# The affine part of the first layer norm computed on GpSimd beside the key scores and kept in DRAM

## The chip, the cores and the metric

The kernel runs on one core of a Trainium2 chip. A core has TensorE (PE in the profile, with its weight loads as PEld), VectorE (DVE), ScalarE (ACT), GpSimd (POOL) and SyncE (SP, which here only issues DMAs). Each engine works through its own queue in order and waits on semaphores. The metric is the device time of one execution in microseconds, lower is better; the median of the runs is what counts.

## What is computed

One layer of a diffusion backbone: differential attention over 512 latent and 256 context tokens, a layer norm, a PEER feed-forward with 16,384 experts, and a second layer norm. Cut to what matters here:

```python
h = layer_norm(DN_ALPHA * h + g1 * o, ln_g[i, 0], ln_b[i, 0])       # o: attention
f = peer_ffn(h * (1.0 + sc2) + sh2, peer_wq[i], peer_keys[i], peer_u[i], peer_v[i])
h = layer_norm(DN_ALPHA * h + g2 * f, ln_g[i, 1], ln_b[i, 1])

def layer_norm(x, g, b):
    mu, var = mean(x), mean((x - mu) ** 2)
    return (x - mu) * rsqrt(var + LN_EPS) * g + b
```

`peer_ffn` scores each token against two sets of 128 sub-keys per head (8 heads), takes the best 16 of each, then the best 16 sums, and mixes the chosen experts. The `h` that enters the second line's norm is the first norm's full output, with its scale `g` and shift `b`: the affine part that this case is about. It is needed only in the last line.

## The kernel before, in words

The 512 tokens are four tiles of 128 (t = 0 to 3), with the 1024 features along a row. Every f32 product is made of three matmuls on a high and a low part (`hi_lo`, lines 135 to 139: ACT writes the high part, DVE or GpSimd the low one; `mm3`, lines 141 to 150).

- `mix` (line 658) makes the first norm. `normed(t)` writes the normed rows without scale and shift to the DRAM tensor `nd[t]`, 512 KB each (line 711).
- `scores` (line 855) is a loop over 16 sets of keys (k). A step has 24 matmuls of 512 columns on weights `qhi`, `qlo`; from k = 4 on GpSimd makes `qlo` (line 882), from weights that SP loads into `qraw` (line 866, two buffers). DVE takes the best 16 of four tiles (`top16`: MAX8, FIND_INDEX8, MATCH_REPLACE8). After step 1 the pool `ag` is made, with five row buffers named `gr`, 512 KB each.
- Tiles 0 to 2 then go through all experts densely (`up`, `down`); tile 3 has its 128 chosen experts gathered one by one into the five `gr` buffers (`fetch` on GpSimd, `gather` on DVE, which adds into `facc`).
- `down` (line 1131) runs over j = 0 to 127, 128 experts each. `prepare(j)` makes the parts `vh`, `vl` (from `vr`) and `wh`, `wl` (from `w`): the high ones on ACT, the low ones on DVE. `accumulate(j)` is 18 matmuls into six PSUM banks. The last five j (TM = 5) are multiplied bank by bank, so that `finish` of a tile can begin while the next is still multiplied: 90 matmuls.
- When the last gather of tile 3 is out, near j = 117, `finish` for tile 3 is put into the queues: `last_rows` loads four rows of norm parameters (scale and shift of both norms, broadcast to 128 partitions) into `gr` buffers, `residual` loads `nd[3]` into the fifth and has GpSimd multiply by the first norm's scale and add its shift (lines 1221, 1222). Tiles 0 to 2 do the same in buffers `h`. `finish` then makes `y = ALPHA * y + gate * f` on DVE (lines 1232, 1233) and the second norm, half of whose affine part is again on GpSimd (lines 1239, 1240; not for tile 2).

A scheduler orders the instructions of each queue, with dependences and priorities of its own; some are pinned to the order in which they are written (`Pinned`, `pin`). A buffer is taken again when its last reader is done, so the load into a `gr` buffer waits for the `gather` that used it.

Of the kernel before, what the change touches and what calls it, by code (L numbers as in the profile page):

```python
# [9 lines left out]
F32 = mybir.dt.float32  # L10
# [10 lines left out]
D = 1024  # L21
# [81 lines left out]
class Net:  # L103
# [5 lines left out]
    def build(self):  # L109
        with ExitStack() as es:  # L110
            self.es = es
            tc = self.tc
            self.cp = es.enter_context(tc.tile_pool(name="cp", bufs=1))
            self.pinned = {}
            self.V = Pinned(self, self.nc.vector)
            self.A = Pinned(self, self.nc.scalar)
            self.T = Pinned(self, self.nc.tensor)
            self.consts()
            for phase in (self.attention, self.mix, self.peer):
                phase()  # L120
                if self.stop == phase.__name__ or self.stop == "route" and phase == self.peer:
                    break
            if self.stop == "attention":
                self.wh.release()
                self.wpool.release()
                self.onpool.release()
            if self.stop == "mix":
                self.u2p.release()
# [529 lines left out]
    def mix(self):  # L658
# [6 lines left out]
        ps = es.enter_context(tc.tile_pool(name="mps", bufs=1, space=PSUM, reuse_waits="tile"))  # L665
        self.dram = self.es.enter_context(tc.tile_pool(name="dram", bufs=1, space=bass.MemoryType.DRAM))
        self.nd = self.dram.tile([NT, 128, D], F32, name="nd")
        self.keys = self.u2p.tile([128, 2, 128], F32, name="keys")
        nc.sync.dma_start(self.keys, a["keysT"])

# [184 lines left out]
    def scores(self):  # L855
# [4 lines left out]
        with tc.tile_pool(name="qp", bufs=1, reuse_waits="tile") as qp:  # L860
# [17 lines left out]
            def split(k):  # L878
                if k < 2 * H:
                    S[k] = [qp.tile([128, KB, 128], FR, name=x, bufs=2) for x in ("qhi", "qlo")]  # L880
                    self.A.activation(S[k][0], RAW[k], AF.Copy)
                    (nc.vector if k < 4 else nc.gpsimd).tensor_tensor(S[k][1], RAW[k], S[k][0].bitcast(F32), op=OP.subtract)  # L882
                    load(k + 2 if k > 3 else 16)

            def product(k):
# [8 lines left out]
            for k in range(2 * H):  # L894
# [14 lines left out]
                if k == 1:  # L909
                    for kb in range(KB):  # L910
                        self.T.transpose(self.row2[:, kb * 128:(kb + 1) * 128], self.u3[:, kb], self.ident)
                    for n in range(2):
                        self.A.activation(self.u2t[:, 512 * n:512 * n + 512], self.row2[:, 512 * n:512 * n + 512], AF.Copy)
                    self.wh.release()
                    self.wpool.release()
                    self.onpool.release()
                    self.ag = self.pes.enter_context(tc.tile_pool(name="ag", bufs=1, side="right", reuse_waits="tile"))
                    self.ug = tc.alloc_tile_pool(name="ug", bufs=1, side="right", reuse_waits="tile")

    def choose(self, t, then=None):  # L920

# [209 lines left out]
    def down(self):  # L1131
# [47 lines left out]

        for j in range(128 - TM):  # L1180
            if at(j - 1) == 256 and not row:
                row += self.last_rows()
                skip[DT] = self.residual(self.ag.tile([128, D], F32, name="gr", bufs=5), DT, row)
                self.finish(self.ag, row, skip, DT, [self.facc[:, :512], self.facc[:, 512:]])
            prepare(j + 2)
            for t in range(DT):
                accumulate(j, t)
            if j + AHEAD in fresh:
                self.up(j + AHEAD)
            self.some(at(j + 1))  # L1190
# [5 lines left out]
        for j in range(130 - TM, 128):  # L1196
            prepare(j, fp if j > 130 - TM else None)
        for t in range(DT):
            skip[t] = self.residual(fp.tile([128, D], F32, name="h", bufs=3), t, row)
        for t in range(DT):  # L1200
            for n in range(2):
                for j in range(128 - TM, 128):
# [3 lines left out]
        vp.release()  # L1206
        ap.release()

    def last_rows(self):

        row = []
        for n in range(4):
            row.append(self.ag.tile([128, D], F32, name="gr", bufs=5))
            self.nc.sync.dma_start(row[n], self.a["ln"][n:n + 1].to_broadcast([128, D]))
        return row

    def residual(self, h, t, row):

        nc = self.nc
        nc.sync.dma_start(h, self.nd[t])  # L1220
        nc.gpsimd.tensor_tensor(h, h, row[0], op=OP.mult)
        nc.gpsimd.tensor_tensor(h, h, row[1], op=OP.add)
        return h

    def finish(self, fp, row, skip, t, f):
# [9 lines left out]
        for i in range(2):  # L1235
            ns = slice(512 * i, 512 * i + 512)
            if i == 1 and t != DT - 1:
                nc.scalar.activation(y[:, ns], y[:, ns], AF.Identity, bias=bias, scale=scale)
                nc.gpsimd.tensor_tensor(y[:, ns], y[:, ns], row[2][:, ns], op=OP.mult)
                nc.gpsimd.tensor_tensor(y[:, ns], y[:, ns], row[3][:, ns], op=OP.add)  # L1240
            else:
                nc.vector.scalar_tensor_tensor(y[:, ns], y[:, ns], mean, row[2][:, ns], op0=OP.subtract, op1=OP.mult)
                nc.vector.scalar_tensor_tensor(y[:, ns], y[:, ns], rstd, row[3][:, ns], op0=OP.mult, op1=OP.add)
            nc.sync.dma_start(self.out[0, t * 128:(t + 1) * 128, ns], y[:, ns])


# [70 lines left out]
```

## Time and profile before

| | |
|---|---|
| median of 3 runs | 1704.1 us (1698.33, 1704.1, 1705.66) |
| the profiled execution, its time | 1702.72 us |
| its span (first to last instruction) | 1700.9 us |
| mean granted TensorE clock | 0.98 of full speed |
| PE busy | 1608.8 us (95%) |
| DVE busy | 1462.5 us (86%) |
| ACT busy | 761.8 us (45%) |
| POOL busy | 646.2 us (38%) |

The rows of the trace are in microseconds from the start of the span. A row of the timeline has the start, the duration, the engine, the line, the operation, what it writes and reads, and in brackets how long the engine had been idle before and what ended that. A helper's instructions carry the helper's line (L97 for those that are pinned, L138 and L139 for `hi_lo`, L146, L148, L149 for the three matmuls of `mm3`). Matmuls are pipelined: the distance between two starts is what one costs, not its duration.

### The profile page before, as it was taken

What the parts mean: (1) busy time and instruction counts of PE and PEld (TensorE: products, weight loads), DVE (VectorE), ACT (ScalarE), POOL (GpSimd) and SP (SyncE); (2) the same over time, 40 slices, a digit from 0 to 9 for tenths busy, and PEclk for the clock granted to TensorE, in tenths of its full rate; (3) what the DMA queues carried; (4) which work ended last, traced back from release to release, by engine and by line L of the source; (5) the groups of instructions that cost most, each with busy time, mean ns of one, the idle gap of its engine ahead of it and who ended that gap; (6) DMA issues with size and microseconds to landing.
All of it is one profiled execution on the core that took longest, in us unless ns stands there. A gap on an engine that the chain in (4) does not pass through costs nothing.

```text
span 1700.9 us, 24498 instructions
## 1 busy us (share of the span) xinstructions
PE 1608.8 (95%) x9057; PEld 1430.2 (84%) x9057; DVE 1462.5 (86%) x2598; ACT 761.8 (45%) x1148; POOL 646.2 (38%) x368
## 2 busy tenths in 40 slices
PE   7899999997999999899999979999999999999977
PEld 3788897876888998899999968888888888888865
DVE  6688897887799999999999468989899789888978
ACT  5475656654333343564666533333333333333322
POOL 1000000000234676327333235655566556655552
PEclk9999999998999999899999989999999999999988
DMA  8765746403222566798999999989899889988952
GB/s 317 192 173 153 180 130 177 151 21 127 89 86 73 177 224 206 266 347 266 333 367 340 331 359 360 378 319 374 322 376 360 336 331 372 362 333 296 356 193 97
DMA packets 134920, 435.92 MB, mean 256 GB/s; under 512 B 13200, under 2 KB 38288, under 8 KB 123408
## 3 DMA queue, kind: packets, MB, share of 16 engines
q1 hardware_dynamic: 75328, 201.02, 34.7%
q0 software_dynamic: 36864, 134.23, 21.2%
q10 hardware_dynamic: 22608, 99.10, 16.6%
q8 instruction: 71, 1.16, 0.3%
q14 instruction: 49, 0.40, 0.1%
HBM read 372.57 MB, written 47.05 MB: 247 GB/s over the span
## 4 chain that ended last, share of the span: by engine, by line
PE 77%; DVE 9%; DMA 6%; issue 4%; ACT 2%; POOL 2%; SPq 0%; ACTq 0%; DVEq 0%; POOLq 0%
PE v L149 11%; PE v L146 10%; PE v L148 10%; PE a L149 10%; PE a L146 10%; PE a L148 9%; PE v L97 3%; PE qkv L146 2%; PE qkv L149 2%; PE qkv L148 2%; DMA adw<-in_ada_b_dram 2%; PE sc L409 2%; DMA qs<-kh 1%; PE mp L228 1%; POOL ulo L1019 1%
## 5 line engine op out<-in xcount | busy, mean ns | idle before, releaser
L146 PE MATMUL a<-u2h,uhi 128*128 128x384 f32 x1024 | 346.7, 339 | 4.5 <-ACT at L97 2.8
L149 PE MATMUL a<-u2h,ulo 128*128 128x384 f32 x1024 | 344.9, 337 | 6.2 <-POOL ulo L1019 4.5
L148 PE MATMUL a<-u2l,uhi 128*128 128x384 f32 x1024 | 343.9, 336 | 0.0
L146 PE MATMUL v<-vh,wh 128*128 128x512 f32 x768 | 300.9, 392 | 9.8 <-ACT wh L138 9.8
L148 PE MATMUL v<-vl,wh 128*128 128x512 f32 x768 | 301.7, 393 | 8.1 <-DVE vl L139 8.1
L149 PE MATMUL v<-vh,wl 128*128 128x512 f32 x768 | 301.7, 393 | 4.6 <-DVE wl L139 4.5
L1095 POOL DMA_INDIRECT gr<-in_peer_u_dram,eidx x128 | 184.3, 1440 | 242.4 <-DVE gr L1104 226.6
L1019 POOL TENSOR_TENSOR ulo<-ur,uhi 128x1024 fp32r<-128x1024 f32 x79 | 210.2, 2666 | 124.2 <-ACT uhi L97 70.1
L138 ACT ACTIVATE vh<-vr 128x1024 fp32r<-128x1024 f32 x128 | 134.6, 1054 | 237.6 <-DMA vr<-in_v_t_dram 96.7
L1095 POOL DMA_INDIRECT gr<-in_peer_v_dram,eidx x128 | 183.1, 1431 | 150.0 <-DVE facc L1111 129.8
L139 DVE TENSOR_TENSOR vl<-vr,vh 128x1024 fp32r<-128x1024 f32 x128 | 164.5, 1286 | 70.6 <-ACT vh L138 70.6
L882 POOL TENSOR_TENSOR qlo<-qraw,qhi 128x1024 fp32r<-128x1024 f32 x12 | 28.8, 2401 | 465.2 <-ACT qhi L97 465.2
L149 PEld LDWEIGHTS a<-u2h,ulo 128*128 128x128 f32 x1024 | 193.2, 189 | 8.5 <-POOL ulo L1019 6.5
L146 PEld LDWEIGHTS a<-u2h,uhi 128*128 128x128 f32 x1024 | 193.3, 189 | 7.1 <-ACT at L97 3.7
L148 PEld LDWEIGHTS a<-u2l,uhi 128*128 128x128 f32 x1024 | 193.4, 189 | 1.5
L1111 DVE SCALAR_TENSOR_TENSOR facc<-gr,act,facc 128x1024 f32<-128x1024 f32 x127 | 184.6, 1453 | 6.1 <-DMA gr<-in_peer_v_dram,eidx 6.1
L146 PEld LDWEIGHTS v<-vh,wh 128*128 128x128 f32 x768 | 145.4, 189 | 39.9 <-ACT wh L138 10.5
L148 PEld LDWEIGHTS v<-vl,wh 128*128 128x128 f32 x768 | 145.6, 190 | 38.6 <-DVE vl L139 8.8
L149 PEld LDWEIGHTS v<-vh,wl 128*128 128x128 f32 x768 | 145.3, 189 | 36.5 <-DVE wl L139 5.9
L97 ACT ACTIVATE at<-a 128x384 f32<-128x384 f32 x90 | 44.2, 492 | 184.7 <-PE a L149 111.3
L139 DVE TENSOR_TENSOR wl<-w,wh 128x384 fp32r<-128x384 f32 x128 | 93.1, 728 | 23.9 <-ACT wh L138 23.5
L138 ACT ACTIVATE wh<-w 128x384 fp32r<-128x384 f32 x128 | 65.1, 517 | 106.7 <-PE v L148 65.7
(269 smaller groups left out, 3257.4 us busy)
## 6 DMA issues: line engine op xcount, KB each, us to landing
ur<-in_u_t_dram SPq DMA_DIRECT2D x128, 512.0 KB, 5.8
vr<-in_v_t_dram ACTq DMA_DIRECT2D x64, 1024.0 KB, 8.2
gq<-gd SPq DMA_DIRECT2D x16, 1536.0 KB, 12.3
gd<-w SPq DMA_DIRECT2D x12, 1920.0 KB, 8.9
ad<-at SPq DMA_DIRECT2D x45, 384.0 KB, 6.3
ar<-ad SPq DMA_DIRECT2D x45, 384.0 KB, 7.3
adw<-in_ada_b_dram ACTq DMA_DIRECT2D x64, 256.0 KB, 3.5
wraw<-in_w_qkv_dram ACTq DMA_DIRECT2D x21, 512.0 KB, 4.2
```

Source lines behind the costliest of these rows:

```text
L97: ins = getattr(self.engine, name)(*args, **kwargs)
L138: (hi_engine or nc.scalar).activation(hi, src, AF.Copy)
L139: return (lo_engine or nc.vector).tensor_tensor(lo, src, hi.bitcast(F32), op=OP.subtract)
L146: ins = nc.tensor.matmul(out, lh, rh, start=first and i == 0, stop=False)
L148: nc.tensor.matmul(out, lh, rl, start=False, stop=False)
L149: ins = nc.tensor.matmul(out, ll, rh, start=False, stop=last and i == n - 1)
L228: nc.tensor.matmul(mp[:2, 2 * i + n], l[:, kb], r[:, ns], start=kb == 0 and k == 0, stop=kb == KB - 1 and k == 2)
L409: nc.tensor.matmul(ps[:, c, n0:n1], QS[h, c][:, v, t * 128:(t + 1) * 128], KS[h, c][:, n0:n1], start=v == 0, stop=v == 1)
L882: (nc.vector if k < 4 else nc.gpsimd).tensor_tensor(S[k][1], RAW[k], S[k][0].bitcast(F32), op=OP.subtract)
L1019: self.paced = (lo_engine or self.nc.gpsimd).tensor_tensor(lo, raw, hi.bitcast(F32), op=OP.subtract)
L1095: ins = nc.gpsimd.indirect_dma_start(out=self.GR[n], out_offset=None, in_=a["peer_v"] if n >= K else a["peer_u"], in_offset=bass.IndirectO ...
L1111: ins = nc.vector.scalar_tensor_tensor(self.facc, r, self.act[:, k:k + 1], self.facc, op0=OP.mult, op1=OP.add)
```

## The change

GpSimd computes `nd[t] * scale + shift` during `scores` and writes it to a new DRAM tensor `hd[t]`; the end loads `hd[t]` in place of `nd[t]` and does nothing further to it. In detail:

- After step 1 of `scores`, the two parameter rows of the first norm are loaded into two `gr` buffers. At k = 3, 5, 7, 9 `nd[t]` is loaded into a third, fourth, fifth and again a freed one. At k = 5, 7, 9, 11 GpSimd multiplies, at k = 6, 8, 10, 12 it adds and issues the DMA to `hd[t]` itself: eight operations of 128x1024 and four stores in all. GpSimd's operations in `scores` are pinned in the order in which they are written.
- At the end `rows(1)` loads only the second norm's two rows, and `residual` is one load.

```diff
@@ -115,6 +115,7 @@
             self.V = Pinned(self, self.nc.vector)
             self.A = Pinned(self, self.nc.scalar)
             self.T = Pinned(self, self.nc.tensor)
+            self.P = Pinned(self, self.nc.gpsimd)
             self.consts()
             for phase in (self.attention, self.mix, self.peer):
                 phase()
@@ -665,6 +666,7 @@
         ps = es.enter_context(tc.tile_pool(name="mps", bufs=1, space=PSUM, reuse_waits="tile"))
         self.dram = self.es.enter_context(tc.tile_pool(name="dram", bufs=1, space=bass.MemoryType.DRAM))
         self.nd = self.dram.tile([NT, 128, D], F32, name="nd")
+        self.hd = self.dram.tile([NT, 128, D], F32, name="hd")
         self.keys = self.u2p.tile([128, 2, 128], F32, name="keys")
         nc.sync.dma_start(self.keys, a["keysT"])
 
@@ -879,7 +881,7 @@
                 if k < 2 * H:
                     S[k] = [qp.tile([128, KB, 128], FR, name=x, bufs=2) for x in ("qhi", "qlo")]
                     self.A.activation(S[k][0], RAW[k], AF.Copy)
-                    (nc.vector if k < 4 else nc.gpsimd).tensor_tensor(S[k][1], RAW[k], S[k][0].bitcast(F32), op=OP.subtract)
+                    (nc.vector if k < 4 else self.P).tensor_tensor(S[k][1], RAW[k], S[k][0].bitcast(F32), op=OP.subtract)
                     load(k + 2 if k > 3 else 16)
 
             def product(k):
@@ -916,6 +918,17 @@
                     self.onpool.release()
                     self.ag = self.pes.enter_context(tc.tile_pool(name="ag", bufs=1, side="right", reuse_waits="tile"))
                     self.ug = tc.alloc_tile_pool(name="ug", bufs=1, side="right", reuse_waits="tile")
+                    row, skip = self.rows(0), []
+                if 3 <= k < 13:
+
+                    t, step = divmod(k - 5, 2)
+                    if k in (3, 5, 7, 9):
+                        skip.append(self.ag.tile([128, D], F32, name="gr", bufs=5))
+                        nc.sync.dma_start(skip[-1], self.nd[len(skip) - 1])
+                    if k > 4:
+                        self.P.tensor_tensor(skip[t], skip[t], row[step], op=(OP.mult, OP.add)[step])
+                        if step:
+                            self.P.dma_start(self.hd[t], skip[t])
 
     def choose(self, t, then=None):
 
@@ -1179,8 +1192,8 @@
 
         for j in range(128 - TM):
             if at(j - 1) == 256 and not row:
-                row += self.last_rows()
-                skip[DT] = self.residual(self.ag.tile([128, D], F32, name="gr", bufs=5), DT, row)
+                row += self.rows(1)
+                skip[DT] = self.residual(self.ag.tile([128, D], F32, name="gr", bufs=5), DT)
                 self.finish(self.ag, row, skip, DT, [self.facc[:, :512], self.facc[:, 512:]])
             prepare(j + 2)
             for t in range(DT):
@@ -1196,7 +1209,7 @@
         for j in range(130 - TM, 128):
             prepare(j, fp if j > 130 - TM else None)
         for t in range(DT):
-            skip[t] = self.residual(fp.tile([128, D], F32, name="h", bufs=3), t, row)
+            skip[t] = self.residual(fp.tile([128, D], F32, name="h", bufs=3), t)
         for t in range(DT):
             for n in range(2):
                 for j in range(128 - TM, 128):
@@ -1206,20 +1219,17 @@
         vp.release()
         ap.release()
 
-    def last_rows(self):
+    def rows(self, i):
 
         row = []
-        for n in range(4):
+        for n in (2 * i, 2 * i + 1):
             row.append(self.ag.tile([128, D], F32, name="gr", bufs=5))
-            self.nc.sync.dma_start(row[n], self.a["ln"][n:n + 1].to_broadcast([128, D]))
+            self.nc.sync.dma_start(row[-1], self.a["ln"][n:n + 1].to_broadcast([128, D]))
         return row
 
-    def residual(self, h, t, row):
-
-        nc = self.nc
-        nc.sync.dma_start(h, self.nd[t])
-        nc.gpsimd.tensor_tensor(h, h, row[0], op=OP.mult)
-        nc.gpsimd.tensor_tensor(h, h, row[1], op=OP.add)
+    def residual(self, h, t):
+
+        self.nc.sync.dma_start(h, self.hd[t])
         return h
 
     def finish(self, fp, row, skip, t, f):
@@ -1236,11 +1246,11 @@
             ns = slice(512 * i, 512 * i + 512)
             if i == 1 and t != DT - 1:
                 nc.scalar.activation(y[:, ns], y[:, ns], AF.Identity, bias=bias, scale=scale)
-                nc.gpsimd.tensor_tensor(y[:, ns], y[:, ns], row[2][:, ns], op=OP.mult)
-                nc.gpsimd.tensor_tensor(y[:, ns], y[:, ns], row[3][:, ns], op=OP.add)
+                nc.gpsimd.tensor_tensor(y[:, ns], y[:, ns], row[0][:, ns], op=OP.mult)
+                nc.gpsimd.tensor_tensor(y[:, ns], y[:, ns], row[1][:, ns], op=OP.add)
             else:
-                nc.vector.scalar_tensor_tensor(y[:, ns], y[:, ns], mean, row[2][:, ns], op0=OP.subtract, op1=OP.mult)
-                nc.vector.scalar_tensor_tensor(y[:, ns], y[:, ns], rstd, row[3][:, ns], op0=OP.mult, op1=OP.add)
+                nc.vector.scalar_tensor_tensor(y[:, ns], y[:, ns], mean, row[0][:, ns], op0=OP.subtract, op1=OP.mult)
+                nc.vector.scalar_tensor_tensor(y[:, ns], y[:, ns], rstd, row[1][:, ns], op0=OP.mult, op1=OP.add)
             nc.sync.dma_start(self.out[0, t * 128:(t + 1) * 128, ns], y[:, ns])
 
 
```

How the queues change (rows of the program's order; names carry the tile's number, no time is in them). First GpSimd, in `scores` around k = 6 to 10: `qlo` is the low part of the key weights, `gr` a row buffer, `hd` the new DRAM tensor. Before:

```order
L882 TENSOR_TENSOR qlo_4693<-qraw_4516,qhi_4692 128x1024
L882 TENSOR_TENSOR qlo_4753<-qraw_4636,qhi_4752 128x1024
L882 TENSOR_TENSOR qlo_4813<-qraw_4696,qhi_4812 128x1024
L882 TENSOR_TENSOR qlo_4873<-qraw_4756,qhi_4872 128x1024
L882 TENSOR_TENSOR qlo_4933<-qraw_4816,qhi_4932 128x1024
```

Now:

```order
L97 TENSOR_TENSOR qlo_4820<-qraw_4701,qhi_4819 128x1024
L97 TENSOR_TENSOR gr_4757<-gr_4757,gr_4633 128x1024
L97 TENSOR_TENSOR qlo_4883<-qraw_4763,qhi_4882 128x1024
L97 TENSOR_TENSOR gr_4757<-gr_4757,gr_4635 128x1024
L97 DMA hd_4144<-gr_4757 128x1024
L97 TENSOR_TENSOR qlo_4945<-qraw_4823,qhi_4944 128x1024
L97 TENSOR_TENSOR gr_4879<-gr_4879,gr_4633 128x1024
L97 TENSOR_TENSOR qlo_5008<-qraw_4886,qhi_5007 128x1024
```

Between two of the weights' low parts stands one more operation, and after every second one a DMA issue.

Second DVE, in `down`, where tile 3 is finished: `facc` is the gathered sum, `gf` that times the gate, `gr` the residual row, and `vl`, `wl`, `w` belong to the j that PE is about to multiply (here j = 119 to 121). Before:

```order
L1232 TENSOR_TENSOR gf_15497<-facc_4500,g2_4501 128x512
L139 TENSOR_TENSOR wl_15525<-w_15523,wh_15524 128x384
L1158 TENSOR_TENSOR w_15583<-gq_15549,at_15344 128x384
L139 TENSOR_TENSOR vl_15520<-vr_15448,vh_15519 128x1024
L1233 SCALAR_TENSOR_TENSOR gr_15490<-gr_15490,gf_15494 128x512
L1233 SCALAR_TENSOR_TENSOR gr_15490<-gr_15490,gf_15497 128x512
L648 BN_STATS fst_15500<-gr_15490 128x6 x2
L139 TENSOR_TENSOR vl_15552<-vr_15547,vh_15551 128x1024
L650 BN_AGGR fm_15503<-fst_15500 128x2
L139 TENSOR_TENSOR wl_15557<-w_15555,wh_15556 128x384
```

Now:

```order
L1242 TENSOR_TENSOR gf_15516<-facc_4501,g2_4502 128x512
L1243 SCALAR_TENSOR_TENSOR gr_15511<-gr_15511,gf_15513 128x512
L1243 SCALAR_TENSOR_TENSOR gr_15511<-gr_15511,gf_15516 128x512
L649 BN_STATS fst_15519<-gr_15511 128x6 x2
L140 TENSOR_TENSOR vl_15539<-vr_15473,vh_15538 128x1024
L651 BN_AGGR fm_15522<-fst_15519 128x2
L140 TENSOR_TENSOR wl_15544<-w_15542,wh_15543 128x384
L652 TENSOR_SCALAR fm_15522<-fm_15522 128x1
L1252 SCALAR_TENSOR_TENSOR gr_15511<-gr_15511,fm_15522,gr_15507 128x512
L1171 TENSOR_TENSOR w_15602<-gq_15568,at_15369 128x384
```

The two operations on the residual row stand ahead of the low parts of j = 119 now, right behind `gf`. On SP, the load into tile 3's `gr` stood fifth in the queue of `gr` buffers (four parameter rows ahead of it) and stands third now (two rows ahead); in `scores` the two rows and three loads of `nd` go ahead of the first loads of expert weights, and the fourth load of `nd` stands ahead of five loads of `qraw`.

## Rows read from the trace of the kernel before

**Rows 1.** Stretches: length, busy (count) of PE, PEld, DVE, ACT, POOL; clock, DMA

```profile
1642.50:1653.40 10.90, 0.93 (x3) 0.29 (x2) 10.90 (x9) 0.00 (x0) 10.27 (x4) 0.74 0.00 1
1653.40:1658.00 4.60, 4.60 (x11) 3.63 (x12) 4.39 (x12) 0.92 (x2) 0.00 (x0) 0.51 0.26 68
...
1670.50:1689.50 19.00, 18.89 (x81) 15.12 (x81) 17.45 (x36) 3.11 (x7) 3.54 (x2) 1.00 0.04 15
```

**Rows 2.** Waits from 1622 to 1676: who waited for whom; total us, times, longest

```profile
PE v L148 <- DVE vl L139: 8.1, 1, 8.1
```

**Rows 3.** Timeline of PE at the end: start us, us, instruction, idle before

```profile
1639.98 0.39 PE L149 MATMUL v<-vh,wl 128*128 128x512 f32 x1
...
1642.25 0.39 PE L146 MATMUL v<-vh,wh 128*128 128x512 f32 x1
1650.78 0.79 PE L148 MATMUL v<-vl,wh 128*128 128x512 f32 x1 [8.14 <-DVE vl L139]
...
1689.05 0.40 PE L149 MATMUL v<-vh,wl 128*128 128x512 f32 x1
```

**Rows 4.** Timeline of SP at the end (loads that it issues)

```profile
1620.49 3.85 SPq L1214 DMA_DIRECT2D gr<-in_ln_dram  x2
1624.45 0.37 SPq L1220 DMA_DIRECT2D h<-nd  x1
...
1628.02 0.33 SPq L1220 DMA_DIRECT2D gr<-nd  x1
```

**Rows 5.** Line 1220 at the end: from issue to landing of its four loads

```profile
DMA to landing us min/median/max: 5.2/6.3/7.3
```

**Rows 6.** Timeline of POOL at the end

```profile
1630.78 2.56 POOL L1221 TENSOR_TENSOR h<-h,gr 128x1024 f32<-128x1024 f32 x1 [15.90 <-DMA h<-nd]
...
1635.98 3.39 POOL L1221 TENSOR_TENSOR gr<-gr 128x1024 f32<-128x1024 f32 x1
1639.44 2.39 POOL L1222 TENSOR_TENSOR gr<-gr 128x1024 f32<-128x1024 f32 x1
...
1649.72 3.21 POOL L1222 TENSOR_TENSOR h<-h,gr 128x1024 f32<-128x1024 f32 x1
...
1659.55 2.15 POOL L1240 TENSOR_TENSOR gr<-gr 128x512 f32<-128x512 f32 x1
```

**Rows 7.** Timeline of DVE at the end

```profile
1628.37 1.29 DVE L1232 TENSOR_TENSOR gf<-facc,g 128x512 f32<-128x512 f32 x2
...
1633.69 3.42 DVE L139 TENSOR_TENSOR vl<-vr,vh 128x1024 fp32r<-128x1024 f32 x1
1641.87 5.57 DVE L1233 SCALAR_TENSOR_TENSOR gr<-gr,gf 128x512 f32<-128x512 f32 x2 [4.76 <-POOL gr L1222]
...
1662.05 1.21 DVE L139 TENSOR_TENSOR vl<-vr,vh 128x1024 fp32r<-128x1024 f32 x1
```

**Rows 8.** Timeline of POOL in the key scores

```profile
447.16 2.40 POOL L882 TENSOR_TENSOR qlo<-qraw,qhi 128x1024 fp32r<-128x1024 f32 x1 [420.60 <-ACT qhi L97]
...
472.70 2.41 POOL L882 TENSOR_TENSOR qlo<-qraw,qhi 128x1024 fp32r<-128x1024 f32 x1 [4.08 <-ACT qhi L97]
479.19 2.41 POOL L882 TENSOR_TENSOR qlo<-qraw,qhi 128x1024 fp32r<-128x1024 f32 x1 [4.09 <-ACT qhi L97]
```

**Rows 9.** Timeline of DVE there: the first MAX8 of three tiles in turn

```profile
447.50 0.27 DVE L97 MAX8 val<-s 128x8 f32<-128x128 f32 x1
...
449.20 0.28 DVE L97 MAX8 val<-s 128x8 f32<-128x128 f32 x1
...
450.91 0.28 DVE L97 MAX8 val<-s 128x8 f32<-128x128 f32 x1
```

**Rows 10.** Timeline of PE there: its first use of the first qlo

```profile
451.82 0.39 PE L149 MATMUL v<-u2h,qlo 128*128 128x512 f32 x1
```

**Rows 11.** Page, groups of instructions: busy us, mean ns of one; idle before

```profile
L1095 POOL DMA_INDIRECT gr<-in_peer_v_dram,eidx x128 | 183.1, 1431 | 150.0 <-DVE facc L1111 129.8
```

**Rows 12.** DMA issues: engine, count, KB each, median us to landing

```profile
gr<-in_peer_v_dram,eidx POOLq DMA_INDIRECT x128, 7.7
...
nd<-x SPq DMA_DIRECT2D x4, 512.0 KB, 2.6
```

## The prediction

> **What bounds the kernel now.** PE is busy 95% of the span, so I asked first where it is not, and went through the windows by stage. Most of the loss that one cause explains lies near the end: from 1642.5 to 1653.4 PE works 0.93 of 10.90 us while DVE and GpSimd are busy nearly throughout, and in the 4.6 us behind it the granted clock is 0.51, the lower of its two levels (1.2 GHz), before it returns [rows 1]. PE had been idle before it fell. The view of waits names the first cause: PE waits 8.1 us for `vl`, the low part of an expert block's rows (j = 120) that DVE makes [rows 2].
>
> Why DVE is late is read backwards. It stood 4.76 us at the residual row of tile 3, and the two operations on that row then took 5.57 us [rows 7]; `vl` of j = 120 is behind them in DVE's queue. The row came from GpSimd, which ended its second operation on it at 1639.44 + 2.39 = 1641.8 [rows 6]. GpSimd had begun at 1630.78, with another tile's row, because that row's load was issued first (1624.45 against 1628.02), and it had waited for that load [rows 4, 6]. So a load, two pairs of GpSimd operations and a slowed DVE stand in series in front of PE.
>
> What PE lost there: from 1642.25 to its last matmul at 1689.05 are 46.8 us [rows 3]. In them it does 17 (rest of j = 120) + 2 x 18 (j = 121, 122) + 90 (the last five) = 143 matmuls. Ten matmuls earlier take 1642.25 - 1639.98 = 2.27 us, so 0.227 each [rows 3]; the last 81 take 18.89 us, 0.233 each [rows 1]. 143 x 0.227 = 32.5, 143 x 0.233 = 33.3, and with 62 at the one and 81 at the other 14.1 + 18.9 = 33.0. Lost: 46.8 - 33.0 = **13.8 us**, 13.5 to 14.3. This takes in the half clock, and a short wait of PE at 1669.5 that the late DVE also feeds.
>
> **The change at the end.** It removes eight GpSimd operations of 128x1024 that run from 1630.78 to 1649.72 + 3.21 = 1652.9 [rows 6] and two of the six 512 KB loads that are made for the finish. The row that DVE wants, now `hd[3]`, is third among the `gr` loads and no longer fifth. The third buffer came free when the second of the two loads at 1620.49 was issued, at 1620.49 + 3.85 - 0.33 = 1624.0 [rows 4]. Loads of this size and place landed in 5.2 to 7.3 us, median 6.3 [rows 5], so the row is there at 1629.2 to 1631.3, say 1630.3. DVE ends the gate product at 1628.37 + 1.29 = 1629.7 [rows 7]. Instead of at 1641.9 it goes on at 1630.3: the wait is all but gone.
>
> The low parts of j = 119 now stand behind the two operations on the row; what is queued there waits for the load and not for GpSimd. Is PE served in time? Two operations on the row cost 1.3 (the undisturbed pair of the same columns [rows 7]), two statistics as much again (estimate), `vl` 1.21 [rows 7], `wl` and `w` of 384 columns 0.45 each (1.21 x 384/1024), some eight small steps of the norm at 0.28, the price of an operation of 128 columns [rows 9], 2.2, the norm's two halves 1.3, then `vl` and `wl` of j = 120, 1.21 + 0.45. Sum 9.9 us: 1630.3 + 9.9 = 1640.2, and PE wants `vl` at 1642.25 + 0.23 = 1642.5. The cover is 2.3 us. Two half-size GpSimd operations of the second norm fall into this stretch (the longer 2.15 [rows 6]) and can take about that from it. I therefore expect PE to run through, with a remainder of 0 to 2 us; I take 0.5. Next to be late would be the last loads of expert rows, which are issued as DVE frees their buffers, now earlier along with it.
>
> Here a rule explains a term. DVE's `vl` took 3.42 us while GpSimd worked and 1.21 when it did not [rows 7]. The Trainium skill, SBUF — State Buffer, Who interferes with whom, says that a DVE instruction with two SBUF inputs and a GpSimd instruction that reads SBUF exclude each other for a whole instruction, and that one with a single input is left alone; the trace agrees at this place. By that rule the moved operations would not touch the scores.
>
> **The change in the scores.** Eight operations of the same form and size as `qlo`, 2.40 us [rows 8], or up to 3.39, the longest of them at the end [rows 6], and four DMA issues on GpSimd. The trace has no direct DMA from GpSimd; its gathers cost it 1.43 us each on the mean [rows 11], zero is the other end, and I take 1.43, the same queue. A period is 479.19 - 472.70 = 6.49 us with 4.09 idle on GpSimd [rows 8]. A period with an add takes 2.40 + 1.43 = 3.83 of these, one with a multiply 2.40: it fits by 0.26 us. With 3.39 it overruns by 0.73 us, and the first `qlo` lay ready at 447.16 + 2.40 = 449.56 while PE used it at 451.82 [rows 8, 10], a cover of 2.26 us. Cost on the path: 0; bounds 0 and, with the cover gone, four overruns of 0.73, 2.9 us. A gain has no reason here: nothing is taken out of this stage.
>
> SP's queue: the rows and three loads of `nd` go ahead of loads that are first used far later, at no cost. The fourth load of `nd` waits for the first store of `hd` (landing: 2.6 us as `nd`'s stores, 7.7 as GpSimd's gathers [rows 12]; I take 2.6, as it is a store of the same size), and five loads of key weights are queued behind it. The store is issued at about 472.70 + 2.41 + 2.40 = 477.5, lands by 480 to 487 (1.43 issue added), and the weights behind it are split two periods after 479.19, at 492.2. At the late end about 5 us are left for one load: covered, though not by much. Cost 0.
>
> **Sum.** 13.8 - 0.5 - 0 = 13.3 us less. The profiled execution took 1702.72 us for a span of 1700.9; its span becomes 1687.6, its time 1689.4. The median of the three runs stands 1.4 us higher, so 1704.1 - 13.3 = 1690.8; I say **1690.5 us**.
>
> **The rivals.**
> (a) The wait comes back in another form: DVE now stands at the load with PE's low parts behind it. For: three low parts are now queued behind the row. Against: the 2.3 us of cover and the landing times. It decides from a landing 2.3 us later than 1630.3; a landing in 12 us instead of 6.3 costs 3.4 us and perhaps 3 more at the half clock, as PE's gap of 10 us is followed by 4.6 us at it. Half the gain is left, 1697. The same time results if PE is held by the loads of the last expert rows.
> (b) Slower: in `scores` GpSimd's eight new operations hold up DVE, as at the end. DVE has no rest there: a tile's selection takes 449.20 - 447.50 = 1.70 us, four of them 6.8, more than PE's period of 6.49, so whatever it loses goes onto the end of the stage. Eight times 2.40 to 3.39 is 19 to 27 us against 13.3 gained: 1710 to 1718. It decides from 13.3 / 8 = 1.7 us of blocking per operation. Against: the same tile's selection beside the `qlo` operation (447.16 to 449.56) took 1.70 us, the next, almost free of it, 450.91 - 449.20 = 1.71 [rows 8, 9].
> (c) The store of `hd[0]` lands late and SP's queue holds up the key weights. It decides from a landing of some 12 us. Each further us stops PE for one, once for the one dependent load; 5 us and a dip of the clock would give 1697. The Trainium skill, DMA: Bandwidth & Descriptors, Anatomy of one DMA, gives 2.0 us plus size over 436 GB/s for a DMA that GpSimd issues, 3.2 us for 512 KB, my estimate from it; by that rule (c) falls, and no run here shows it.
> (d) The change doesn't do what it says: it does, by the order of the queues: no such operation of GpSimd is left in front of DVE's row.
>
> **How the numbers follow.** Forecast 0.77, (a) 0.13, (b) 0.05, (c) 0.05. The forecast's own range, with 13.5 to 14.3 lost, a remainder of 0 to 2 and 0 to 2.9 in the scores, is a gain of 8.6 to 14.3: 1690 to 1695.5 from the median, and from the fastest run shown (1698.33) down to 1684. To 1698 it takes in (a) and (c) and leaves out (b). Range 1685 to 1698. 0.5% is 8.5 us, about what a measurement of this kernel can tell from no change: faster than 1695.6 is the forecast and a part of (a), 0.80; within 0.5% the rest of (a) and (c) and the milder half of (b), 0.16; slower 0.04.
>
> **What would show it.** In the changed profile: no GpSimd operation between about 1614 and the second norm's halves; `gr<-hd` issued near 1624 and DVE's first operation on it within 1 us of its landing, the pair in 1.3 us; no idle time of PE above 1 us and a clock of 1.00 from 1640 to its last matmul, near 1675; in the scores a period of 6.49 us and selections of 1.70 us. Wrong it is if PE waits there for `vl` again, if the scores end later than in the kernel before, or if the first stretch of `down` begins later.

## The result, and the profile after

The changed kernel took 1686.8 us (median of 4 runs) against 1704.2 us: ratio 0.9896, 95% interval 0.9861 to 0.9931. Measured again beside other kernels on one chip it took 1689.1 us against 1701.3: 0.9928, 0.9906 to 0.9951. The forecast was 1690.5 us.

In the trace the place of the gain can be read to a tenth of a microsecond. Its last stretch lies between two matmuls that every kernel here has: the last on `a` (the experts' first product) and the last on `v`. In the kernel before, the latter starts at 1689.05 [rows 3], and the former (timeline of PE, columns as there) is

```profile
1625.71 0.33 PE L149 MATMUL a<-u2h,ulo 128*128 128x384 f32 x1
```

and in the changed kernel (timeline of PE):

```profile
1623.48 0.33 PE L150 MATMUL a<-u2h,ulo 128*128 128x384 f32 x1
...
1672.65 0.40 PE L150 MATMUL v<-vh,wl 128*128 128x512 f32 x1
```

63.34 us became 49.17: **14.17 us**, the whole lost time that the prediction had put at 13.8. I call this length the last stretch from here on. The spans differ by 16.4 us; the other 2.2 are not the change's: the first matmul on key weights, before any changed instruction, already stood 1.87 us earlier in this trace (434.74 against 436.61), and 1.05 us later (437.66) in the second trace of the changed kernel.

Windows of the changed kernel, the same columns as in [rows 1]:

```profile
1623.50:1642.50 19.00, 19.00 (x85) 15.73 (x84) 17.67 (x29) 8.59 (x12) 3.51 (x2) 1.00 0.62 223
1642.50:1653.40 10.90, 10.90 (x50) 9.02 (x49) 6.77 (x11) 4.78 (x6) 0.00 (x0) 1.00 0.53 201
1653.40:1672.60 19.20, 19.20 (x85) 15.74 (x84) 17.30 (x36) 3.70 (x8) 2.96 (x2) 1.00 0.04 15
```

PE is busy throughout, and the granted clock is 1.00 where it had been 0.51. SP, POOL and DVE there (timelines; they answer to [rows 4, 6, 7]):

```profile
1621.78 0.32 SPq L1232 DMA_DIRECT2D gr<-hd  x1
```
```profile
1634.75 2.02 POOL L1249 TENSOR_TENSOR gr<-gr 128x512 f32<-128x512 f32 x1 [22.09 <-ACT gr L1248]
1636.84 1.49 POOL L1250 TENSOR_TENSOR gr<-gr 128x512 f32<-128x512 f32 x1
```
```profile
1626.14 1.28 DVE L1242 TENSOR_TENSOR gf<-facc,g 128x512 f32<-128x512 f32 x2
1627.34 1.28 DVE L1243 SCALAR_TENSOR_TENSOR gr<-gr,gf 128x512 f32<-128x512 f32 x2
...
1634.40 1.22 DVE L140 TENSOR_TENSOR vl<-vr,vh 128x1024 fp32r<-128x1024 f32 x1
1635.53 1.65 DVE L140 TENSOR_TENSOR wl<-w,wh 128x384 fp32r<-128x384 f32 x1
1637.23 2.19 DVE L140 TENSOR_TENSOR vl<-vr,vh 128x1024 fp32r<-128x1024 f32 x1
```

DVE goes from the gate product to the residual row without a wait, the pair takes 1.28 us, and `wl` of j = 120 is done at 1637.2, 9.8 us after the row was taken up. GpSimd appears only for the second norm's halves, and there two operations of DVE are long again: 1.65 and 2.19 us for forms that take 0.5 and 1.21.

In the scores GpSimd works as forecast and nothing else moves (timeline of POOL, and of SP for the load that waits for the first store):

```profile
470.83 2.41 POOL L97 TENSOR_TENSOR qlo<-qraw,qhi 128x1024 fp32r<-128x1024 f32 x1 [1.75 <-ACT qhi L97]
473.19 2.40 POOL L97 TENSOR_TENSOR gr<-gr 128x1024 f32<-128x1024 f32 x1
475.90 0.76 POOL L97 DMA_DIRECT2D hd<-gr  x1 [0.32 <-PE v L97]
```
```profile
479.06 0.33 SPq L927 DMA_DIRECT2D gr<-nd  x1
```

From the first to the last matmul on key weights it is 91.54 us, before 91.53.

### The profile page after: what moved, and what is told of

It reads as the page before. It is cut to its first block, busy times and chain, and to the rows that moved or that the text cites. A ratio compares the mean times of both kernels' runs of the same rounds, so it can differ in the third digit from the quotient of the medians.

```text
span 1684.5 us, 24512 instructions
## 1 busy us (share of the span) xinstructions
PE 1603.2 (95%) x9057; PEld 1426.6 (85%) x9057; DVE 1449.5 (86%) x2598; ACT 762.4 (45%) x1148; POOL 643.9 (38%) x372
## 4 chain that ended last, share of the span: by engine, by line
PE 76%; DVE 10%; DMA 7%; issue 4%; ACT 2%; POOL 1%; SPq 0%; ACTq 0%; DVEq 0%; POOLq 0%
PE v L150 10%; PE v L149 10%; PE v L147 10%; PE a L150 9%; PE a L147 9%; PE a L149 9%; PE v L97 3%; PE qkv L150 2%; PE qkv L147 2%; PE qkv L149 2%; PE sc L410 2%; DMA adw<-in_ada_b_dram 2%; PE mp L229 1%; DMA ad<-at 1%; DMA qs<-kh 1%
## 5 line engine op out<-in xcount | busy, mean ns | idle before, releaser
L140 DVE TENSOR_TENSOR wl<-w,wh 128x384 fp32r<-128x384 f32 x128 | 89.4, 699 | 24.4 <-ACT wh L139 23.0
```

The costliest lines, as they stand in the source:

```text
L140: return (lo_engine or nc.vector).tensor_tensor(lo, src, hi.bitcast(F32), op=OP.subtract)
```

## The experiments

My theory at the start was the prediction's: tile 3's row came late out of a chain of loads and GpSimd operations, and DVE's queue carried the lateness to PE. The rival was that GpSimd's presence beside DVE is the cost, whichever row it works on. The changed kernel, `end_only`, `tile3_moved`, `load_first` and `tiles012_moved` have the same order on DVE in the last stretch; the rest are said apart.

### One half of the change each

`scores_only`: `row` at the end is `self.rows(0) + self.rows(1)`, and `residual` is that of the kernel before. 

> Only the part of the change that lies in the scores: the eight GpSimd operations, the loads of rows and the four stores to hd are made as in the changed kernel, but the end does all of its old work and does not read hd. My theory (the added work is hidden in GpSimd's idle time): the scores last as long as before, 91.5 us from the first to the last matmul on key weights, the end still loses its 13.8 us, and the time is that of before, ratio 0.998 to 1.002. Rival (GpSimd's new operations hold up DVE or delay qlo): 1 to 3 us more by delay of qlo, 19 to 27 us more by blocking, all of it between the first and the last such matmul.

Ratio 1.0008 (0.9993 to 1.0023), last stretch 63.46 us, scores 91.55.

`end_only`: the block `if 3 <= k < 13` is taken out, and `residual` loads `nd` and leaves out the scale and shift. 

> Only the part at the end: nothing is added to the scores, and the end loads nd and uses it as it is, so the scale and shift of the first norm are left out of the last line. My theory: the whole gain is made at the end, so the time is that of the changed kernel, ratio 0.988 to 0.993, and PE has no wait over 1 us from 20 us before the last expert weights to its last matmul. Rival (the early computation takes part in the gain, or costs something that the changed kernel pays and this one does not): a time 2 us or more away from the changed kernel's, with a different length of the scores.

Ratio 0.9933 (0.9909 to 0.9956), last stretch 49.17 us, the changed kernel's to the hundredth. So the work in the scores costs nothing that these runs can tell, and the gain is made wholly at the end. These agree with both theories of why.

### Tile 3 alone, and the order alone

```diff
# tile3_moved: in scores only nd[3] -> hd[3] (k = 3 to 6); at the end
+                first = self.rows(0)        # behind rows(1) and tile 3's load
...
-            skip[t] = self.residual(fp.tile([128, D], F32, name="h", bufs=3), t)
+            skip[t] = fp.tile([128, D], F32, name="h", bufs=3)
+            nc.sync.dma_start(skip[t], self.nd[t])
+            nc.gpsimd.tensor_tensor(skip[t], skip[t], first[0], op=OP.mult)
+            nc.gpsimd.tensor_tensor(skip[t], skip[t], first[1], op=OP.add)
```

> Only tile 3's affine part is moved into the scores; tiles 0 to 2 keep their six GpSimd operations at the end, none of them ahead of tile 3's row. DVE's order is that of the changed kernel. Theory of the queue (DVE was late because its row came late from GpSimd): DVE finds the row ready and PE runs through, time of the changed kernel, 1687 to 1690. Theory of the shared port (GpSimd's work next to DVE's operations of two inputs makes these longer, as the pair of 5.57 us and the vl of 3.42 us in the kernel before): operations between the row and vl of j = 120 take up to twice as long, 20 us instead of 10 with a cover of about 3, PE waits 3 to 7 us, 1691 to 1697.

```diff
# load_first: the kernel before, with the rows of the second norm behind tile 3's load
-                row += self.last_rows()
+                row += self.rows(0)
                 skip[DT] = self.residual(..., DT, row)
+                row += self.rows(1)
```

> Nothing is moved into the scores; only the order at the end differs: tile 3's nd is loaded third and not fifth, its two GpSimd operations stand ahead of those of the other tiles, and DVE's order is that of the changed kernel. From the changed kernel's trace: load issued 5.5 us before DVE wants the row, then two operations of 2.4 to 3.4, so DVE waits 5 to 7 us instead of 0; with some 3 us of cover PE waits 2 to 4, and with the half clock behind it 5: 1690 to 1695 by the queue alone. If GpSimd's later operations also lengthen DVE's, 3 to 7 us more: 1694 to 1702. If only removing the operations helps and their order is of no account: 1702 to 1705.

Measured: 0.9989 (0.9974 to 1.0004) and 1.0019 (1.0000 to 1.0037); last stretches 60.88 (1627.36 to 1688.24) and 62.47 us (1624.60 to 1687.07). Next to nothing, although in `tile3_moved` DVE has its row at once. This is where my theory fell. The timelines of POOL and DVE in `tile3_moved`:

```profile
1633.19 2.39 POOL L1212 TENSOR_TENSOR h<-h,gr 128x1024 f32<-128x1024 f32 x1 [16.65 <-DMA gr<-in_ln_dram]
1635.96 2.95 POOL L1213 TENSOR_TENSOR h<-h,gr 128x1024 f32<-128x1024 f32 x1 [0.38 <-DMA gr<-in_ln_dram]
1638.86 2.72 POOL L1212 TENSOR_TENSOR h<-h,gr 128x1024 f32<-128x1024 f32 x1
...
1644.34 2.65 POOL L1212 TENSOR_TENSOR h<-h,gr 128x1024 f32<-128x1024 f32 x1
1647.07 2.34 POOL L1213 TENSOR_TENSOR h<-h,gr 128x1024 f32<-128x1024 f32 x1
```
```profile
1631.22 1.29 DVE L1244 SCALAR_TENSOR_TENSOR gr<-gr,gf 128x512 f32<-128x512 f32 x2
1632.42 1.28 DVE L649 BATCH_NORM_STATS2 fst<-gr 128x6 f32<-128x512 f32 x2
1633.62 3.04 DVE L140 TENSOR_TENSOR vl<-vr,vh 128x1024 fp32r<-128x1024 f32 x1
1636.58 0.20 DVE L651 BATCH_NORM_AGGREGATE fm<-fst 128x2 f32<-128x12 f32 x1
1636.70 2.63 DVE L140 TENSOR_TENSOR wl<-w,wh 128x384 fp32r<-128x384 f32 x1
1639.25 0.14 DVE L652 TENSOR_SCALAR fm<-fm 128x1 f32<-128x1 f32 x1
1639.32 2.81 DVE L1253 SCALAR_TENSOR_TENSOR gr<-gr,fm 128x512 f32<-128x512 f32 x1
1642.05 2.74 DVE L1168 TENSOR_TENSOR w<-gq,at 128x384 f32<-128x384 f32 x1
1644.71 0.15 DVE L654 RECIPROCAL fm<-fm 128x1 f32<-128x1 f32 x1
1644.90 2.10 DVE L156 SCALAR_TENSOR_TENSOR fm<-fm 128x1 f32<-128x1 f32 x1
1647.04 0.16 DVE L157 TENSOR_TENSOR fm<-fm 128x1 f32<-128x1 f32 x1
1647.23 2.19 DVE L158 SCALAR_TENSOR_TENSOR fm<-fm 128x1 f32<-128x1 f32 x1
```

Nearly every DVE operation with two tensor inputs stands until the GpSimd operation beside it has ended, and only then does its own work: `wl` ends 0.4 us behind the GpSimd operation that ends at 1638.91, and `fm` (128x1 elements, 0.16 us in the changed kernel) takes 2.10 and ends at 1647.00, GpSimd's at 1646.99. Those with one input (statistics, their aggregation, the reciprocal, `TENSOR_SCALAR`) keep their time in between. Six operations are longer by 3.04 - 1.21, 2.63 - 0.50, 2.81 - 0.74, 2.74 - 0.55, 2.10 - 0.16 and 2.19 - 0.16, in sum 12.2 us, out of the 14.3 (6 x 2.38, the time of such an operation in the scores) that GpSimd's work there takes by itself.

How that reaches PE is read on ACT, which works in order too. It stands at tile 3's norm until DVE's small `fm` operations are through, and `wh`, which PE wants, is queued behind (timeline of ACT, then the waits of PE):

```profile
1649.65 0.81 ACT L1249 ACTIVATE gr<-gr,fm 128x512 f32<-128x512 f32 x1 [9.07 <-DVE fm L656]
1650.37 0.51 ACT L139 ACTIVATE wh<-w 128x384 fp32r<-128x384 f32 x1
```
```profile
PE v L147 <- ACT wh L139: 6.9, 1, 6.9
```

These 6.9 us are in the 3 to 7 that the rival expected, but its time, 1691 to 1697, was missed too (1698.9). It had left out what follows: one more wait of 0.8 us, and some 4 us (the rest of the 11.7 that this kernel loses) that go with the lower granted clock. After PE's idle time it is 0.50 from 1652.0 to 1657.0, and matmuls start 0.43 us apart there and not 0.23.

In `load_first` DVE stood 4.78 us for the row, like the 4.76 in [rows 7], and its pair took 5.64 us like the 5.57 (timeline of DVE): the order of the loads was not the matter.

```profile
1633.33 5.64 DVE L1234 SCALAR_TENSOR_TENSOR gr<-gr,gf 128x512 f32<-128x512 f32 x2 [4.78 <-POOL gr L1223]
```

### The counterpart: tiles 0 to 2 moved, tile 3 left

```diff
# tiles012_moved: in scores 3 <= k < 11 (three tiles); at the end
-                row += self.rows(1)
-                skip[DT] = self.residual(self.ag.tile([128, D], F32, name="gr", bufs=5), DT)
+                first = self.rows(0)
+                skip[DT] = self.ag.tile([128, D], F32, name="gr", bufs=5)
+                nc.sync.dma_start(skip[DT], self.nd[DT])
+                nc.gpsimd.tensor_tensor(skip[DT], skip[DT], first[0], op=OP.mult)
+                nc.gpsimd.tensor_tensor(skip[DT], skip[DT], first[1], op=OP.add)
+                row += self.rows(1)
```

> The counterpart of moving tile 3 alone: tiles 0 to 2 are moved into the scores, tile 3 keeps its load of nd (third) and its two GpSimd operations at the end; DVE's order is that of the changed kernel. Theory of exclusion (each DVE operation of two inputs lasts until the GpSimd operation beside it has ended, so it is GpSimd's presence there that costs): after tile 3's two operations GpSimd is idle, DVE waits about 5 us for the row, then needs 9.8 us to wl of j = 120 as in the changed kernel; with a cover of 3, PE waits 1.5 to 3 us: 1687 to 1693. Theory of the late row (my prediction's chain): tile 3's row is as late as in the run with its load first, so the time is that run's, 1698 to 1702.

0.9941 (0.9921 to 0.9961), last stretch 52.05 us (1624.26 to 1676.31): 80% of the gain, with tile 3's row as late as ever. DVE's timeline and PE's only waits there:

```profile
1633.67 1.30 DVE L1247 SCALAR_TENSOR_TENSOR gr<-gr,gf 128x512 f32<-128x512 f32 x2 [5.47 <-POOL gr L1199]
1634.88 1.28 DVE L649 BATCH_NORM_STATS2 fst<-gr 128x6 f32<-128x512 f32 x2
1636.08 1.21 DVE L140 TENSOR_TENSOR vl<-vr,vh 128x1024 fp32r<-128x1024 f32 x1
```
```profile
PE v L150 <- DVE wl L140: 1.1, 1, 1.1
PE v L149 <- DVE vl L140: 0.2, 1, 0.2
```

DVE waits longer for its row than in the kernel before, 5.47 us, and PE loses 2.9 us in place of 14.2. The late row is worth the smaller part; the six operations of the tiles that nobody waits for are worth the larger. `load_first` differs from it by these six operations alone in the last stretch: there DVE takes the row up 8.7 us after the last matmul on `a`, here 9.4, and the stretches are 62.47 and 52.05 us. The two loads fewer that the changed kernel makes at the end are not the gain either: `tiles012_moved` makes all eight, as `tile3_moved` does.

### The same work in quarters

In the two kernels above (tile 3 moved; load first) each GpSimd operation becomes four:

```diff
-nc.gpsimd.tensor_tensor(h, h, row[i], op=...)
+for n in range(4):
+    ns = slice(256 * n, 256 * n + 256)
+    nc.gpsimd.tensor_tensor(h[:, ns], h[:, ns], row[i][:, ns], op=...)
```

> As the run that moves tile 3 alone, but each of the six remaining GpSimd operations is made as four of 128x256: the same work in quarters. Exclusion by whole instructions: a DVE operation waits for a quarter, 0.6 us, instead of 2.0 (12.2 us over six operations there); the stretch from the residual's first operation to wl of j = 120 shrinks from 21.8 to 13 to 15 us, against the 12.8 that PE leaves: 1688 to 1693. If DVE and GpSimd merely share bandwidth, the total is unchanged and the time is that of the unsplit run, 1697 to 1700.

> Nothing is moved into the scores; tile 3's load is third and its operations first, as in the run with its load first, and each of the eight GpSimd operations is made as four of 128x256. Exclusion by whole instructions: DVE still waits 4.8 us for the row, then 3 to 5 us for quarters instead of 12: PE loses 4 to 8 us instead of 14, 1692 to 1697. Shared bandwidth: as the unsplit run, 1699 to 1703. It would beat the changed kernel only if the whole loss were the length of GpSimd's operations, 1685 to 1688.

0.9997 (0.9978 to 1.0015) and 1.0009 (0.9991 to 1.0026), last stretches 62.62 and 64.90: no gain, and the times that I expected from the exclusion were wrong; they came out near those of the theory of shared bandwidth. The waits are the exclusion's all the same: in `tile3_quarters` a DVE operation now waits for a quarter only (groups of DVE from 1639.2 to 1665.5, then GpSimd's operations):

```profile
L140 DVE TENSOR_TENSOR vl<-vr,vh 128x1024 fp32r<-128x1024 f32 x6 | 10.0, 1663 | 0.0
L140 DVE TENSOR_TENSOR wl<-w,wh 128x384 fp32r<-128x384 f32 x6 | 6.4, 1070 | 0.0
...
L158 DVE SCALAR_TENSOR_TENSOR fm<-fm 128x1 f32<-128x1 f32 x1 | 0.7, 662 | 0.0
```
```profile
1640.63 26.90 POOL L1215 TENSOR_TENSOR h<-h,gr 128x256 f32<-128x256 f32 x24 [18.46 <-DMA gr<-in_ln_dram]
```

`vl` takes 1.66 and not 3.04, `fm` 0.66 and not 2.1. From the residual's first operation (1638.03) to the end of `wl` of j = 120 (1651.44) it is 13.4 us, within the 13 to 15 expected, and PE waits 1.1 us for j = 120 where it had waited 7.6. The two engines take turns for 26.9 us in place of 16, so more operations wait: six `vl` (0.45 each), six `wl` (0.57), five `w` (0.5), two halves of the norm (1.0 together) and four `fm` (0.47) are 11.5 us, against 12.2. The sum hardly changes, but it is spread over more of the last j.

Most of what PE loses comes behind that, by another wait (timelines of DVE and PE, and a wait of SP):

```profile
1673.74 0.56 DVE L1168 TENSOR_TENSOR w<-gq,ar 128x384 f32<-128x384 f32 x1 [7.49 <-DMA ar<-ad]
1676.63 1.22 PE L149 MATMUL v<-vl,wh 128*128 128x512 f32 x2 [6.09 <-DVE vl L140]
SPq L1257 <- POOL gr L1253: 20.9, 1, 20.9
```

The second norm's two GpSimd operations are queued behind the quarters and begin at 1667.50. SP's second store of tile 3's output waits 20.9 us for them, and behind it in SP's queue stands the load of `ar` (the activated first product of the last two j, kept in DRAM), which goes out at 1670.58. DVE stands idle for it, and PE waits 6.1 us of its 9.6 for the `vl` behind that. `load_first_quarters` has the same chain: DVE idle for 5.0 us, a wait of PE of 4.1. So these two runs show that DVE waits for one whole operation of GpSimd, and not that cutting is useless; what the quarters would give without that wait stays open.

### The work on DVE itself

If that is so, DVE should do the work: an operation costs it 1.21 us of its own instead of 2.4 of standing.

```diff
# end_on_dve: load_first with
-        nc.gpsimd.tensor_tensor(h, h, row[0], op=OP.mult)
-        nc.gpsimd.tensor_tensor(h, h, row[1], op=OP.add)
+        nc.vector.tensor_tensor(h, h, row[0], op=OP.mult)
+        nc.vector.tensor_tensor(h, h, row[1], op=OP.add)
```

> Nothing is moved into the scores; tile 3's load is third and the eight operations of the affine part at the end are made by DVE and not by GpSimd. Theory of exclusion (while DVE is never idle there, each us that GpSimd works is one that DVE does not, however the work is cut): an operation costs DVE its own 1.21 us instead of the 2.4 that it stands still for GpSimd; eight cost 9.7 instead of about 12 to 19, the row is ready 2.4 us after its landing, and with a cover of 3 us the stretch from the last matmul on a to the last on v is 52 to 58 us, against 62.5 with GpSimd and 49.2 in the changed kernel; the time is 1689 to 1697. If GpSimd's work ran beside DVE's at a fair share, taking it back to DVE would cost DVE all 9.7 us: 63 us or more, no gain.

0.9938 (0.9917 to 0.9960), 1689.4 us, last stretch 51.02 us, a little better than my lower end. But the scheduler puts the operations on tiles 0 to 2 among those for j = 120 to 124, until 31 us after the last matmul on `a`; GpSimd's in `load_first` end after 25 us, and in the changed kernel DVE has slack only from j = 122 on. So two things differ, the engine and the place. That an operation takes DVE 1.21 us is seen; how much of the gain is due to that, and whether the other theory's 63 us stayed away for the place alone, is not shown. Nothing is moved into the scores, no DRAM tensor is added, and all but 1.9 us of the gain is there. The times of this kernel and of the changed one can't be told apart (1689.4 and 1689.1).

### Why the scores bear it

```diff
# scores_two_input: in scores, behind top16 of each tile
+                    if 5 <= k < 13:
+                        self.V.tensor_tensor(s[:, t], s[:, t], s[:, t], op=OP.mult)
# double_pool: the line self.P.tensor_tensor(skip[t], skip[t], row[step], ...) stands twice
```

> The changed kernel with one more DVE operation behind each tile's selection in steps 5 to 12 (32 operations, the product of the tile's used-up 128x128 scores with themselves, whose result nothing reads): an operation that reads two inputs, in the place where the selections read one. Exclusion: those that fall beside a GpSimd operation (4.8 of each 6.49 us) last until it has ended, up to 2.4 us, 0.9 to 1.3 us on the mean of all 32, and the selections end 20 to 40 us later than in the changed kernel. If the scores were free because they have room, and not because of the kind of operation: 0.15 to 0.25 us each, 5 to 8 us in all.

> The changed kernel with each of the eight GpSimd operations in the scores made twice (the rows in hd, and so the output, are then scaled and shifted twice). GpSimd then needs 2.40 + 2 x 2.38 = 7.2 us, every second step 0.6 more for the store, against the period of 6.49: about 1.0 us over for eight steps, 8 us, of which its present idle time ahead of the first and the cover of qlo (2.3 us, one step's worth of buffer more at most) take 2 to 5: the scores last 3 to 6 us longer than 91.5, and the selections of DVE still take 1.70 us each. If GpSimd's operations held up DVE there: 19 us or more.

Each was run once. In `scores_two_input` the 32 operations, with the selections' own beside them (groups of DVE there):

```profile
L97 DVE FIND_INDEX8 idx<-val,s 128x8 uint32<-128x128 f32 x127 | 36.2, 285 | 0.0
L97 DVE MAX8 val<-s 128x8 f32<-128x128 f32 x126 | 36.2, 287 | 2.2
L97 DVE TENSOR_TENSOR s<-s 128x128 f32<-128x128 f32 x32 | 27.1, 848 | 1.1
L97 DVE MATCH_REPLACE8 s<-val,s 128x128 f32<-128x128 f32 x63 | 17.4, 276 | 0.0
```

They take 0.85 us on the mean, up to 2.53, a little under my 0.9 to 1.3; the selections keep their 0.28 to 0.29 us, end 28.6 us later, and the run took 1712.7 us. Where GpSimd is idle such an operation takes 0.29 us, so 9.3 of the 27.1 us are their own work and 17.8 are standing: seven that start as a `qlo` operation runs stand 15.2 us together, seven that meet the end of a moved operation 2.5. So the place is free because of the kind of operation that DVE has there. That rival (b)'s 19 to 27 us would have come with another kind is not shown: most of the standing is beside `qlo`, which the kernel before has too.

In `double_pool` the scores last 98.48 us, 6.9 more, just over the 3 to 6 expected; PE waits 5.3 us for `qlo` and the selections are not slowed. GpSimd's room in this stage thus holds the 20 operations of the changed kernel (12 `qlo`, 8 moved) and not 28. The run's 1690.1 us, one value, doesn't tell this from the changed kernel; the trace does. About half of the 6.9 is made up again before the end: from the first matmul on key weights to the last on `a` it is 1192.2 us, against 1188.7 and 1186.4 in the changed kernel's two traces.

### The changed kernel again

> The changed kernel once more, for its size beside the others on the same chip and for a second trace. Both theories: 0.988 to 0.993 of the kernel before, PE without a wait of over 1 us in the last 50 us, scores of 91.5 us from the first to the last matmul on key weights.

0.9928 (0.9906 to 0.9951), no wait of PE in the last stretch, 49.17 us.

## Why the prediction came out right, and where its reasons did not

- **The size.** Lost time 13.8 us by the count of matmuls; 14.17 measured. It was the whole loss that had to be found and not its parts, and the remainder that I left in (0.5 us) is zero. The price of 0.233 us for the last matmuls was too high (85 take 19.20 us in the changed kernel, 0.226 each); by the other, 0.227, the loss is 14.3.
- **The cause, wrong.** The step that failed is the one that read DVE's lateness backwards as "a load, two pairs of GpSimd operations and a slowed DVE" in series, with DVE's 4.76 us at the row at its head. Taking that wait away entirely (`tile3_moved`) gave back 2.5 us of 14.2; leaving it and taking the other tiles' operations away (`tiles012_moved`) gave back 11.3. What stood in its place was DVE itself, which waits for the end of the GpSimd operation beside it, 12.2 us over six of its own. The row's place in SP's queue, third and not fifth, was worth 0.9 (`load_first`). The forecast held, by luck as far as the cause goes, because the change removes all eight operations (and two of eight loads, not of the six that I counted); for a change that moved only the row that is waited for, the same reasoning would have forecast some 13 us and been wrong.
- **The rule that I used for one term carries most of the loss.** The pair of 5.57 us and the `vl` of 3.42 in [rows 7] were such waits for a whole GpSimd operation. The Trainium skill, SBUF — State Buffer, Who interferes with whom, says what `tile3_moved` shows: DVE operations with two SBUF inputs and GpSimd operations that read SBUF hold each other off for a whole instruction, and one-input ones go on. What the runs add is the price: in a stretch where DVE is hardly idle, 14.3 us of GpSimd's work cost DVE 12.2 us, and 11.5 when it was cut in quarters.
- **DVE's chain.** 9.9 us were summed up to `wl` of j = 120, 9.8 measured; two errors cancel in it. The small steps of the norm take 0.14 to 0.20 us each and not 0.28, and `wl` of j = 120, beside GpSimd's half of the second norm, took 1.65 and not 0.45. The cover of PE, put at 2.3 us, was 3.1: PE was to want it at 1642.5, 2.2 earlier in this trace, 1640.3, and it was done at 1637.2.
- **The load.** Issue at 1624.0 was forecast; 1621.78 is that, 2.2 us earlier as all is here. It had landed after 5.6 us at most (1627.34), the short end of [rows 5], so DVE did not wait the 0.6 us that I gave it. Rival (a) did not come.
- **The scores.** Cost 0, as forecast, with the selections as the reason; `scores_only` and `scores_two_input` show both. GpSimd's own issue of a DMA takes 0.6 to 0.76 us and not the 1.43 of a gather [rows 11].
- **The store.** SP's next load went out at 479.06, 3.2 us after the store's issue began at 475.90, near the 2.6 that I took and far from the 12 that rival (c) needed. The load waited for that store (SP's waits: `SPq L927 <- DMA hd<-gr: 5.4, 1, 5.4`). The estimate of 3.2 us from the Trainium skill (DMA: Bandwidth & Descriptors, Anatomy of one DMA) agrees.

## What to carry to other kernels

Before work is handed to GpSimd to spare DVE, look at what DVE does in that stretch: beside operations of two inputs on a DVE that has no idle time, each microsecond of GpSimd cost DVE 0.8 to 0.85 here, and the same operation takes DVE itself half as long (1.21 against 2.38 us); beside one-input operations such as MAX8 or the statistics it cost nothing. Look too at what is queued behind that work: in the quarters it was a store, and behind the store a load that PE needed. In a trace the sign is a DVE operation whose duration is far from that of its form elsewhere, the small ones above all (2.1 us for 128x1 elements), ending where a GpSimd operation ends. A wait that stands at the head of a chain is not yet its cause: move it alone and see, and move the rest alone and see.

## What was not expected of the hardware

The exclusion was seen on DVE operations from 128x1 to 128x1024, and in both directions. In `end_on_dve` a GpSimd operation of 128x512, 1.26 us elsewhere, took 7.22 while DVE worked through low parts and rows without a pause (timeline of POOL):

```profile
1642.12 7.22 POOL L1240 TENSOR_TENSOR gr<-gr 128x512 f32<-128x512 f32 x1 [30.55 <-ACT gr L1239]
```

It ended at 1649.34, 1.15 us after DVE first had nothing to do there (1648.19). Why DVE and GpSimd take strict turns in most places, and GpSimd is passed over for several DVE operations here, these runs do not show.
